# Queries and keys of the mixer made already turned, a pair of heads at a time, behind values and pooled channels

## Chip, core and metric

The kernel runs on one core of a Trainium2 chip. The metric is the device time of one execution in microseconds (us), lower is better. Engines are named as the profile names them: PE (TensorE) for matrix products, with PEld for its weight loads, DVE (VectorE), ACT (ScalarE), POOL (GpSimd), and SP, which issues most of the transfers.

## What is computed

A decoder layer on 256 tokens of width 1024: a SwiGLU FFN (width 2816), a token mixer, a second FFN, each with RMS normalisation and with shift, scale and gate from a conditioning vector.

```python
h = h + 0.5 * gt1 * swiglu(modulate(rmsnorm(h, g_ffn1), sh1, sc1), w1_gate, w1_up, w1_down)
n = modulate(rmsnorm(h, g_mix), sh2, sc2)
u, q, k, v = split(n @ w_in)                 # 512 columns each
y_pool = multiscale_pool(u, w_pool, pool_scale)   # 4 groups of 128 channels, windows 2, 4, 8, 16
y_attn = dilated_attention(q, k, v)               # 8 heads of 64, causal, ALiBi, 3 dilated branches
h = h + gt2 * (concat([y_pool, y_attn]) @ w_out)
h = h + 0.5 * gt3 * swiglu(modulate(rmsnorm(h, g_ffn2), sh3, sc3), w2_gate, w2_up, w2_down)
return rmsnorm(h, g_final)
```

## The kernel before

The 256 tokens are two tiles (t = 0, 1) of 128. Every large product is made of three products in a rounded 32-bit type: each operand is split into a high part and a rest, and hi*hi, lo*hi and hi*lo are summed. Weights come as units of 1 MB (128 x 2048 floats), in the order that `plan()` writes out; SP loads them into four buffers (`raw`), and for each half of a unit ACT makes the high part (L293) and DVE the rest (L294). A unit of kind "ada" is not a weight of PE: DVE reduces it with the conditioning vector, two reductions a unit (L282, with its read-out), to columns of shift, scale and gate. `weave` puts these units between the others; `WMIX` says from which unit of the mixer on. A load waits until the buffer that it takes is free, which means DVE is done with it.

The order on each engine is written by a scheduler from the code's order and from priorities (`urgent`); `order_dep` and `line_up` add orders by hand around the normalisations.

The mixer begins with the normalised tokens, turned so that the model width is on partitions: `nm[t]`, as high part and rest. They live in one of three homes (`homes`, `new_n`): two in `rounded`, one in `third`; the mixer's result `y[t]` takes a home too. `zchunk(ci, t)` makes 512 columns of `w_in` for one token tile: the tokens are the stationary operand, 512 columns of weights stream, 24 products of 512 rows, then ACT copies the result out (L742). Chunks come in the order q0, k0, q1, k1, v0, v1, u0, u1. `turn_heads(t)` turns q and k of a tile (eight PE transposes, L321, names `tq`, `tk`) and ACT copies them to `qT`, `kT` (L847). For a pair of heads hp, `scores` makes the products (PE, L760, `sc`), DVE adds the bias and takes the minimum (L771), ACT the exponential (L773), DVE divides (L775, L777); `heads_turn` turns the probabilities (L787, `pt`, copied by ACT at L790 to `pts`), `heads_out` multiplies them with the values (L799, `yt`), and ACT and DVE write high part and rest to y (L802, L804). These steps stand between products of the later chunks. `pool_group(g)` makes two small products and writes y (L810 to L823). `wout(t, ...)` is the output product (L890, `accm`), 48 products a tile. `finish2(t)` adds the gated result to `h` (L343, L345), sums squares on ACT (L348) and DVE (L351), and POOL takes the root (L354); ACT and DVE scale the rows (L356, L357, `xsc`), PE turns them (`xtc`), and the second FFN's first products (`le`, L522) begin.

In the FFNs, from chunk 6 (first) and 4 (second) on, `block` works the other way: 128 columns of weights are stationary, and `rounded` streams for both tiles at once, 512 rows (high part and rest of both tiles) against the weights' high part and 256 against their rest.

Of the kernel before, what the change touches and what calls it, by code (L numbers as in the profile page):

```python
# [15 lines left out]
P = 128  # L16
S = 256
# [25 lines left out]
WMIX = (4, 12)  # L43
# [16 lines left out]
def plan():  # L60
# [33 lines left out]
    mix = [("win", (ci, h)) for ci in (1, 2, 3, 0) for h in range(2)] + [("wout", i) for i in WOUT]  # L94
# [8 lines left out]
def pack(inp):  # L103
# [14 lines left out]
    for i, (kind, a) in enumerate(order):  # L118
# [58 lines left out]
def block_kernel(ctx, tc, w, vec, x, c, gf, wpool, bandd, biasd, out):  # L177
# [150 lines left out]
    homes = iter((0, 1, 2, 1, 2, 0, 0, 1))  # L328
# [106 lines left out]
    def block(f, ci, b, hh, hl):  # L435

        his, los = want("gu", (f, ci, b))
        ps = [psp.tile([P, 2 * S], F32, name=f"bl{f}_{ci}_{b}{e}", tag="ps") for e in range(2)]
        for k in range(KD):
            for e in range(2):  # L440
                mm(ps[e], his[k // 4][:, ts(k % 4 * 2 + e, P)], rounded[:, k].rearrange("p a t c -> p (a t c)"),  # L441
                   start=k == 0, stop=False)
        for k in range(KD):
            for e in range(2):
                mm(ps[e][:, 0:S], los[k // 4][:, ts(k % 4 * 2 + e, P)], rounded[:, k, 0].rearrange("p t c -> p (t c)"),  # L445
                   start=False, stop=k == KD - 1)
        with urgent():
# [246 lines left out]
    def finish1(t):  # L694
        with urgent():
            if t == 0:
                scale_cols(1, SC2)
            xs = norm_rows(t, f"b{t}", nm["acc"][t], nm["g"],
                           (place["win", (1, 1)] + 0.5 if t == 0 else place["win", (3, 0)], place["win", (1, 0)] + 1))
        def after(steps, gate=GATE):  # L700
            nm[t] = norm_mod(xs, 1, SH2, f"b{t}", step=steps[gate])
            if t == 1:
                r0, m0, r1, m1 = [chain[f"b{u}", kind] for u in range(NT) for kind in ("rows", "mod")]
                soon = [halves_of([("win", (1, 1)), ("win", (2, 0))], e)[1:] for e in range(2)]
                late = [halves_of([("win", (2, 1))], e) for e in range(2)]
# [24 lines left out]
    def zchunk(ci, t, scale=1.0, between={}):  # L730
# [10 lines left out]
        with urgent():  # L741
            nc.scalar.activation(z, ps, AF.Copy, scale=scale)  # L742
# [51 lines left out]
    def heads_out(hp, v, y):  # L794
        pts = turned_p[hp]
        ps = psp.tile([P, S], F32, name=f"yt{hp}", tag="ps")
        for t, cs, qs in ((0, slice(0, S), slice(0, S)), (1, slice(P, S), slice(S, 384))):
            for e in range(2):
                mm(ps[e * DH:e * DH + DH, cs], v[t][:, ts(2 * hp + e, DH)], pts[e][:, qs], start=t == 0, stop=t == 1)  # L799
        with urgent():  # L800
            for t in range(NT):
                nc.scalar.copy(y[t][0][:, slot(t, 4 + hp), :], ps[:, ts(t, P)])  # L802
            for t in range(NT):
                nc.vector.tensor_tensor(y[t][1][:, slot(t, 4 + hp), :], ps[:, ts(t, P)],  # L804
                                        y[t][0][:, slot(t, 4 + hp), :].bitcast(F32), ALU.subtract)

    def pool_group(g, u, y):
# [10 lines left out]
        with urgent():  # L818
            sc = psc[:, g:g + 1]
            for t in range(NT):  # L820
                nc.scalar.activation(y[t][0][:, slot(t, g), :], p2[:, ts(t, P)], AF.Copy, scale=sc)
            for t in range(NT):
                nc.vector.scalar_tensor_tensor(y[t][1][:, slot(t, g), :], p2[:, ts(t, P)], sc,  # L823
                                               y[t][0][:, slot(t, g), :].bitcast(F32), ALU.mult, ALU.subtract)
# [87 lines left out]
    wout(0, (0, 1))  # L912
# [91 lines left out]
```

## Time and profile before

| what | value |
|---|---|
| time, median of 3 runs (lowest to highest) | 475.97 us (475.29 to 476.56) |
| the profiled execution's own time | 478.23 us |
| its span, first to last instruction | 476.4 us |
| PE busy | 465.5 us (98%) |
| DVE busy | 372.3 us (78%) |
| ACT busy | 276.1 us (58%) |
| granted TensorE clock, mean | 0.996 |
| mixer, first w_in product to first product of the second FFN | 200.64 to 285.15 us |

The busy times are shares of the whole span. In rows of the timeline the first column is the start from the span's start, the second the length; consecutive matmuls overlap, so the time that one takes of PE is the distance to the next start. "x8" is a run of eight like it. A bracket says how long the engine was idle before the row, and what ended that.

### The profile page before, as it was taken

What the parts mean: (1) busy time and instruction counts of PE and PEld (TensorE: products, weight loads), DVE (VectorE), ACT (ScalarE), POOL (GpSimd) and SP (SyncE); (2) the same over time, 40 slices, a digit from 0 to 9 for tenths busy, and PEclk for the clock granted to TensorE, in tenths of its full rate; (3) what the DMA queues carried; (4) which work ended last, traced back from release to release, by engine and by line L of the source; (5) the groups of instructions that cost most, each with busy time, mean ns of one, the idle gap of its engine ahead of it and who ended that gap; (6) DMA issues with size and microseconds to landing.
All of it is one profiled execution on the core that took longest, in us unless ns stands there. A gap on an engine that the chain in (4) does not pass through costs nothing.

```text
span 476.4 us, 6380 instructions
## 1 busy us (share of the span) xinstructions
PE 465.5 (98%) x2327; PEld 387.7 (81%) x2327; DVE 372.3 (78%) x616; ACT 276.1 (58%) x488; POOL 13.5 (3%) x35
## 2 busy tenths in 40 slices
PE   8899999999999999999999999999999999999994
PEld 4678888888888888888878888888888888888883
DVE  4988899997989995689999868967876766666344
ACT  4666586444556563886877478847545554655211
POOL 1000000000000000120001000000000000000010
PEclk9999999999999999999999999999999999999998
DMA  8999896799789976568986974986678755550002
GB/s 280 421 342 354 286 362 256 291 411 420 268 310 378 352 281 246 207 216 327 378 295 258 371 259 178 369 316 252 229 270 296 264 177 182 191 203 1 2 4 84
DMA packets 19105, 126.09 MB, mean 265 GB/s; under 512 B 2217, under 2 KB 2753, under 8 KB 4738
## 3 DMA queue, kind: packets, MB, share of 16 engines
q1 hardware_dynamic: 17568, 121.18, 67.4%
q0 software_dynamic: 1216, 3.98, 2.4%
q10 hardware_dynamic: 290, 0.53, 0.3%
q8 instruction: 18, 0.29, 0.2%
q14 instruction: 13, 0.11, 0.1%
HBM read 124.62 MB, written 1.06 MB: 264 GB/s over the span
## 4 chain that ended last, share of the span: by engine, by line
PE 79%; DMA 7%; DVE 5%; ACT 5%; issue 2%; SPq 1%; POOL 1%; POOLq 0%; DVEq 0%; ACTq 0%
PE accf L473 22%; PE bl L441 18%; PE bl L445 10%; PE le L522 9%; DMA raw<-in_w_dram 7%; PE ld L522 6%; PE accm L890 5%; ACT hi L293 2%; PE sh L405 2%; PE ld L405 2%; DVE lo L294 1%; DVE raw L282 1%; PE ht L427 1%; PE sh L406 1%; PE ld L406 1%
## 5 line engine op out<-in xcount | busy, mean ns | idle before, releaser
L294 DVE TENSOR_TENSOR lo<-raw,hi 128x1024 fp32r<-128x1024 f32 (+1 forms) x158 | 184.2, 1193 | 40.8 <-ACT hi L293 24.2
L293 ACT CAST hi<-raw 128x1024 fp32r<-128x1024 f32 (+1 forms) x158 | 158.8, 1031 | 66.7 <-DMA raw<-in_w_dram 35.0
L441 PE MATMUL bl<-rounded,hi 128*128 128x512 f32 x384 | 91.5, 390 | 0.0
L282 DVE CUSTOM_DVE_ANT_0 raw<-raw,cb,h 128x1024 f32<-128x1024 f32 x70 | 88.2, 1278 | 2.2 <-DMA raw<-in_w_dram 2.2
L441 PEld LDWEIGHTS bl<-rounded,hi 128*128 128x128 f32 x384 | 71.1, 188 | 14.1
L473 PE MATMUL accf<-hi,hh 128*128 128x512 f32 x172 | 54.5, 392 | 0.0
L473 PE MATMUL accf<-hi,hl 128*128 128x512 f32 x172 | 54.1, 390 | 0.0
L473 PE MATMUL accf<-lo,hh 128*128 128x512 f32 x172 | 54.0, 389 | 0.0
L445 PEld LDWEIGHTS bl<-rounded,lo 128*128 128x128 f32 x384 | 49.2, 191 | 1.9
L445 PE MATMUL bl<-rounded,lo 128*128 128x256 f32 x384 | 49.8, 283 | 0.0
L473 PEld LDWEIGHTS accf<-lo,hh 128*128 128x128 f32 x172 | 32.3, 188 | 6.8
L473 PEld LDWEIGHTS accf<-hi,hl 128*128 128x128 f32 x172 | 32.2, 188 | 6.7
L473 PEld LDWEIGHTS accf<-hi,hh 128*128 128x128 f32 x172 | 31.5, 188 | 5.9
L522 PE MATMUL le<-hi,rounded 128*128 128x512 f32 x128 | 32.4, 390 | 0.0
L451 ACT COPY sg<-bl 128x256 f32<-128x256 f32 x24 | 8.9, 373 | 37.5 <-PE bl L445 37.5
L522 PE MATMUL ld<-hi,rounded 128*128 128x512 f32 x112 | 29.1, 397 | 0.7 <-ACT rounded L500 0.7
L522 PEld LDWEIGHTS le<-hi,rounded 128*128 128x128 f32 x128 | 24.0, 188 | 4.9
L522 PEld LDWEIGHTS ld<-hi,rounded 128*128 128x128 f32 x112 | 20.7, 188 | 6.9 <-ACT rounded L500 2.1
L405 PE MATMUL zp<-hi,third 128*128 128x512 f32 x64 | 20.3, 398 | 0.0
L405 PE MATMUL zp<-hi,rounded 128*128 128x512 f32 x64 | 20.1, 396 | 0.0
L453 ACT ACTIVATE sg<-sg 128x256 f32<-128x256 f32 x24 | 10.1, 420 | 14.9 <-DVE sg L452 14.7
L522 PE MATMUL le<-lo,rounded 128*128 128x512 f32 x64 | 17.6, 389 | 0.0
(195 smaller groups left out, 556.5 us busy)
## 6 DMA issues: line engine op xcount, KB each, us to landing
raw<-in_w_dram SPq DMA_DIRECT2D x112, 1024.0 KB, 6.2
raw<-in_w_dram SPq DMA_DIRECT2D x4, 512.0 KB, 8.4
gt<-gd POOLq DMA_DIRECT2D x3, 512.0 KB, 6.9
bias<-in_bias_dram POOLq DMA_DIRECT2D x2, 512.0 KB, 3.7
h<-in_x_dram SPq DMA_DIRECT2D x1, 576.0 KB, 4.6
band_all<-in_band_dram POOLq DMA_DIRECT2D x1, 544.0 KB, 4.8
h<-in_x_dram SPq DMA_DIRECT2D x1, 512.0 KB, 3.7
gfb<-in_gf_dram POOLq DMA_DIRECT2D x1, 512.0 KB, 11.2
```

Of the source, the lines that this page charges most:

```text
L282: note(nc.vector.tensor_tensor_reduce(r, r, cb, 1.0, vecs[:, m:m + 1], ALU.mult, ALU.add, mod[:, m:m + 1]), i, 1)
L293: note(nc.scalar.copy(hi[:, o:o + n], src), i + s / 2, 0)
L294: note(nc.vector.tensor_tensor(lo[:, o:o + n], src, hi[:, o:o + n].bitcast(F32), ALU.subtract), i + s / 2, 0)
L405: return [mm(ps, nh[:, k, :], whi, start=first, stop=False), mm(ps, nl[:, k, :], whi, start=False, stop=False), mm(ps, nh[:, k, :], wlo, s ...
L406: mm(ps, nh[:, k, :], wlo, start=False, stop=last)]
L441: mm(ps[e], his[k // 4][:, ts(k % 4 * 2 + e, P)], rounded[:, k].rearrange("p a t c -> p (a t c)"), start=k == 0, stop=False)
L445: mm(ps[e][:, 0:S], los[k // 4][:, ts(k % 4 * 2 + e, P)], rounded[:, k, 0].rearrange("p t c -> p (t c)"), start=False, stop=k == KD - 1)
L451: nc.scalar.copy(dst, src[:, S:2 * S])
L453: nc.scalar.activation(sg, sg, AF.Silu)
L473: steps.append(mm(accs[b], a, cols(ww, 2 * k + b), start=st, stop=sp))
L522: done.append(mm(banks[ci][t], n[t][a][:, j, :], cols(ww, lead_set(f, j).index(ci)), start=j == 0 and p == 0, stop=last and p == 2))
L890: steps.append(mm(acc2[t][b], a[:, slot(t, k), :], cols(ww, 2 * kk + b), start=st, stop=sp))
```

## The change

Values and pooled channels come first, as chunks like before: v0, u0, v1, u1. Queries and keys follow as four blocks of the FFN's kind (`heads_in(hp)`): a unit "qk" holds the 128 columns of q and the 128 columns of k of one pair of heads; weights stay, and `rounded` streams for both tiles, so q and k come out turned. ACT copies the half that comes of the tokens' rest, scaled, and DVE adds the other half onto it into `qT`, `kT`. The attention steps of pairs 0 to 2 stand between the two halves of later blocks; the rest of them between pool groups and inside `wout(0)`. Since blocks read `rounded` for both tiles, `nm` takes the homes 0 and 1; y of tile 0 takes home 0 after that, y of tile 1 takes `third`, and the first heads' y of tile 0, written before the last block is done, has a tile of its own (`y_first`). The modulation units come one place earlier in the weight order.

```diff
-WMIX = (4, 12)
+WMIX = (3, 11)
...
-    mix = [("win", (ci, h)) for ci in (1, 2, 3, 0) for h in range(2)] + [("wout", i) for i in WOUT]
+    mix = [("win", (ci, h)) for ci in (3, 0) for h in range(2)] + [("qk", hp) for hp in range(4)]
+    mix += [("wout", i) for i in WOUT]
...
+        elif kind == "qk":
+            w[i].reshape(P, KD, 2, P)[:] = win[:, :, :, 1:3, P * a:P * a + P].transpose(2, 0, 1, 3, 4).reshape(P, KD, 2, P)
...
-    homes = iter((0, 1, 2, 1, 2, 0, 0, 1))
+    homes = iter((0, 1, 0, 0, 2, 1, 0, 1))
...
+    def weights_stay(unit, ps, between=None):
+        his, los = unit
         for k in range(KD):
             for e in range(2):
                 mm(ps[e], his[k // 4][:, ts(k % 4 * 2 + e, P)], rounded[:, k].rearrange("p a t c -> p (a t c)"),
                    start=k == 0, stop=False)
+        if between:
+            between()
         for k in range(KD):
             for e in range(2):
                 mm(ps[e][:, 0:S], los[k // 4][:, ts(k % 4 * 2 + e, P)], rounded[:, k, 0].rearrange("p t c -> p (t c)"),
                    start=False, stop=k == KD - 1)
...
-    def turn_heads(t):
-        def go():
-            pts = [turn(z[f"{name}{t}"], f"t{name}{t}") for name in "qk"]
-            with urgent():
-                for dst, pt in zip((qT, kT), pts):
-                    nc.scalar.copy(dst[:, :, ts(t, P)], pt)
...
-    z["q0"] = zchunk(1, 0, QS)
-    z["k0"] = zchunk(2, 0, 1.0, {AFTER1: lambda: after(nm["steps"], 5)})
-    z["q1"] = zchunk(1, 1, QS, {3: turn_heads(0)})
-    z["k1"] = zchunk(2, 1, 1.0)
-    z["v0"] = zchunk(3, 0, 1.0, {3: turn_heads(1), 6: go((0, 0), (0, 1))})
-    z["v1"] = zchunk(3, 1, 1.0)
-    z["u0"] = zchunk(0, 0, 1.0, {1: go((1, 0)), 3: go((2, 0), (0, 2)), 7: go((1, 1))})
-    z["u1"] = zchunk(0, 1, 1.0, {1: go((2, 1), (0, 3)), 4: go((1, 2)),
-                                 6: lambda: (go((2, 2))(), nm.update(g2=gate_rows(GT2, 1.0)))})
-    for g in range(4):
-        pool_group(g, (z["u0"], z["u1"]), y)
-        if g == 1:
-            heads_turn(3)
-    heads_out(3, (z["v0"], z["v1"]), y)
+    y_first = xp.tile([P, 2, P], F32R, name="y_first")
+    def yk(t, k, e):
+        return y_first[:, e, :] if (t, k) == (0, 4) else y[t][e][:, k, :]
...
+    def heads_in(hp, between=None):
+        ps = [accp.tile([P, 2 * S], F32, name=f"qk{hp}{e}", tag="acc") for e in range(2)]
+        weights_stay(want("qk", hp), ps, between)
+        with urgent():
+            for e, (dst, scale) in enumerate(((qT, QS), (kT, 1.0))):
+                tmp = work.tile([P, S], F32, name=f"qk_rest{hp}{e}", tag="t2", bufs=T2)
+                nc.scalar.activation(tmp, ps[e][:, S:2 * S], AF.Copy, scale=scale)
+                nc.vector.scalar_tensor_tensor(dst[:, hp, :], ps[e][:, 0:S], scale, tmp, ALU.mult, ALU.add)
...
+    z["v0"] = zchunk(3, 0)
+    z["u0"] = zchunk(0, 0, {AFTER1: lambda: after(nm["steps"], 5)})
+    z["v1"] = zchunk(3, 1)
+    z["u1"] = zchunk(0, 1)
+    heads_in(0)
+    heads_in(1, go((scores, 0)))
+    heads_in(2, go((heads_turn, 0), (scores, 1)))
+    heads_in(3, go((heads_out, 0), (heads_turn, 1), (scores, 2)))
+    nm["g2"] = gate_rows(GT2, 1.0)
+    for g in range(2):
+        pool_group(g)
+    go((heads_out, 1), (heads_turn, 2), (scores, 3))()
+    for g in range(2, 4):
+        pool_group(g)
+    heads_out(2)
...
-    wout(0, (0, 1))
+    wout(0, (0, 1), None, {2: lambda: heads_turn(3), 3: lambda: heads_out(3)})
```

What the scheduler makes of it, at three places. First PE, where q and k of tile 1 were turned before (inside the chunk v0; `tq`, `tk` are the transposes):

```order
L406 MATMUL zp_2134<-lo_1_1780,third 128x512
L321 MATMUL tq_2158<-ident,z_2105 128x128 x4
L321 MATMUL tk_2163<-ident,z_2132 128x128 x4
L405 MATMUL zp_2134<-hi_1_1779,third 128x512 x2
L406 MATMUL zp_2134<-lo_1_1780,third 128x512
```

and now, in the second block (`qk_2181`, `qk_2182` are its q and k), where the scores of pair 0 stand between high and low weights:

```order
L443 MATMUL qk_2181<-rounded,hi_1_1942 128x512
L443 MATMUL qk_2182<-rounded,hi_1_1942 128x512
L769 MATMUL sc_2213<-kT,qT 128x128
L769 MATMUL sc_2214<-kT,qT 128x128
L769 MATMUL sc_2213<-kT,qT 128x256
L769 MATMUL sc_2214<-kT,qT 128x256
L449 MATMUL qk_2181<-rounded,lo_0_1939 128x256
L449 MATMUL qk_2182<-rounded,lo_0_1939 128x256
```

The transposes are gone, and what stands between the products is the scores, which need DVE's additions of the block before.

Second, the last pair's scores. On PE they stood ahead of the last pooled chunk's later products (`yt_2404` is `heads_out(1)`, `sc` the scores of pair 3):

```order
L799 MATMUL yt_2404<-pts_2387,z_2255 64x256
L799 MATMUL yt_2404<-pts_2393,z_2255 64x256
L799 MATMUL yt_2404<-pts_2387,z_2282 64x128
L799 MATMUL yt_2404<-pts_2393,z_2282 64x128
L760 MATMUL sc_2413<-kT,qT 128x128
L760 MATMUL sc_2414<-kT,qT 128x128
L760 MATMUL sc_2413<-kT,qT 128x256
L760 MATMUL sc_2414<-kT,qT 128x256
L405 MATMUL zp_2400<-hi_0_1959,rounded 128x512 x2
```

and now they stand between pool groups, behind three early output products (`accm`) and the turn of pair 2:

```order
L808 MATMUL yt_2488<-pts_2398,z_2098 64x128
L808 MATMUL yt_2488<-pts_2404,z_2098 64x128
L796 MATMUL pt_2497<-ident,p_2412 128x128 x3
L796 MATMUL pt_2503<-ident,p_2423 128x128 x3
L898 MATMUL accm_2573<-hi_0_2051,third 128x512 x2
L898 MATMUL accm_2572<-lo_0_2052,third 128x512
L769 MATMUL sc_2509<-kT,qT 128x128
L769 MATMUL sc_2509<-kT,qT 128x256
L769 MATMUL sc_2510<-kT,qT 128x128
L769 MATMUL sc_2510<-kT,qT 128x256
L819 MATMUL po_2537<-band_all,z_2071 128x128
```

Scores of pair 3 now follow `heads_out(1)` by a turn and three products. On DVE, the subtraction of `heads_out(1)` (`yt_2404`) and the minima of pair 3 (`p_2419`) stood behind one cast:

```order
L294 TENSOR_TENSOR lo_0_2180<-raw_2177,hi_0_2179 128x1024
L804 TENSOR_TENSOR rounded<-yt_2404,rounded 128x128
L804 TENSOR_TENSOR third<-yt_2404,third 128x128
L771 ISA p_2419,mx_2420<-sc_2413,bias_1921 128x128
L771 ISA mx_2420 128x1
L771 ISA p_2430,mx_2431<-sc_2414,bias_1921 128x128
```

and now (`yt_2488`, `p_2515`) behind two pool groups' subtractions, a reduction and a cast:

```order
L832 SCALAR_TENSOR_TENSOR rounded<-pw_2470,psc,rounded 128x128
L832 SCALAR_TENSOR_TENSOR third<-pw_2470,psc,third 128x128
L285 ISA raw_2183,mod<-raw_2183,cb,h 128x1024
L285 ISA mod 128x1
L832 SCALAR_TENSOR_TENSOR rounded<-pw_2482,psc,rounded 128x128
L832 SCALAR_TENSOR_TENSOR third<-pw_2482,psc,third 128x128
L297 TENSOR_TENSOR lo_0_2272<-raw_2269,hi_0_2271 128x1024
L813 TENSOR_TENSOR rounded<-yt_2488,rounded 128x128
L813 TENSOR_TENSOR third<-yt_2488,third 128x128
L780 ISA p_2515,mx_2516<-sc_2509,bias_1925 128x128
L780 ISA mx_2516 128x1
```

So between the pools and the minima DVE has more to do than before. 

Third, the third normalisation. DVE, the residual of tile 0 (`resc`) up to its sum of squares (L351) and the scaled rows (L357):

```order
L343 TENSOR_TENSOR resc_2676<-accm_2566,gt_2483 128x512
L343 TENSOR_TENSOR resc_2682<-accm_2567,gt_2483 128x512
L345 TENSOR_TENSOR h<-h,resc_2676 128x512
L345 TENSOR_TENSOR h<-h,resc_2682 128x512
L386 SCALAR_TENSOR_TENSOR acol<-mod,gains 128x1
L351 ISA resc_2682,vc_2685<-h,vc_2679 128x512
L351 ISA vc_2685 128x1
L357 TENSOR_SCALAR xsc_2690<-h,rc_2687 128x512
```

and now, where the same lines are L346 to L360:

```order
L346 TENSOR_TENSOR resc_2705<-accm_2570,gt_2462 128x512
L346 TENSOR_TENSOR resc_2711<-accm_2571,gt_2462 128x512
L348 TENSOR_TENSOR h<-h,resc_2705 128x512
L348 TENSOR_TENSOR h<-h,resc_2711 128x512
L285 ISA raw_2574,mod<-raw_2574,cb,h 128x1024
L285 ISA mod 128x1
L354 ISA resc_2711,vc_2714<-h,vc_2708 128x512
L354 ISA vc_2714 128x1
L285 ISA raw_2600,mod<-raw_2600,cb,h 128x1024
L285 ISA mod 128x1
L360 TENSOR_SCALAR xsc_2719<-h,rc_2716 128x512
```

Three reductions that stood ahead of the residual stand inside its chain or after it. On ACT, from the first products' inputs of the second FFN to tile 1's scaled rows (L348 the square, L356 the rows):

```order
L293 CAST hi_0_2629<-raw_2627 128x1024
L500 ACTIVATE rounded<-xT_2570,mod,acol 128x128 x2
L293 CAST hi_1_2633<-raw_2627 128x1024
L348 ACTIVATE resc_2763,vc_2766<-h 128x512
L356 ACTIVATE xsc_2776<-h,rc_2774 128x512
```

and now (L351 the square, L359 the rows):

```order
L509 ACTIVATE rounded<-xT_2703,mod,acol 128x128 x2
L296 CAST hi_0_2644<-raw_2642 128x1024
L351 ACTIVATE resc_2792,vc_2795<-h 128x512
L296 CAST hi_1_2648<-raw_2642 128x1024
L359 ACTIVATE xsc_2805<-h,rc_2803 128x512
```

One cast that stood ahead of the square stands behind it.

More of the change, by code (lines that the diff above doesn't have):

```diff
@@ L446, in block @@
                    start=False, stop=k == KD - 1)
+    def block(f, ci, b, hh, hl):
+        ps = [psp.tile([P, 2 * S], F32, name=f"bl{f}_{ci}_{b}{e}", tag="ps") for e in range(2)]
+        weights_stay(want("gu", (f, ci, b)), ps)
         with urgent():
@@ L698, in finish1 @@
             xs = norm_rows(t, f"b{t}", nm["acc"][t], nm["g"],
-                           (place["win", (1, 1)] + 0.5 if t == 0 else place["win", (3, 0)], place["win", (1, 0)] + 1))
+                           (place["win", (3, 1)] + 0.5 if t == 0 else place["qk", 0], place["win", (3, 0)] + 1))
         def after(steps, gate=GATE):
@@ L703, in after @@
                 r0, m0, r1, m1 = [chain[f"b{u}", kind] for u in range(NT) for kind in ("rows", "mod")]
-                soon = [halves_of([("win", (1, 1)), ("win", (2, 0))], e)[1:] for e in range(2)]
-                late = [halves_of([("win", (2, 1))], e) for e in range(2)]
+                soon = [halves_of([("win", (3, 1)), ("win", (0, 0))], e)[1:] for e in range(2)]
+                late = [halves_of([("win", (0, 1))], e) for e in range(2)]
                 line_up(r0[0], *soon[0], m0[0], *late[0], r1[0], m1[0])
@@ L728, in block_kernel, with zchunk @@
     xp = mix_pool.__enter__()
[L730 removed]
+    def zchunk(ci, t, between={}):
         ps, steps = accp.tile([P, 512], F32, name=f"zp{ci}{t}", tag="acc"), []
@@ L741, in zchunk @@
         with urgent():
-            nc.scalar.activation(z, ps, AF.Copy, scale=scale)
+            nc.scalar.copy(z, ps)
         return z
@@ L792, in heads_turn, with heads_out @@
         turned_p[hp] = pts
-    def heads_out(hp, v, y):
+    def heads_out(hp):
         pts = turned_p[hp]
@@ L866, in block_kernel @@
-    for g in range(4):
-        pool_group(g, (z["u0"], z["u1"]), y)
-        if g == 1:
-            heads_turn(3)
-    heads_out(3, (z["v0"], z["v1"]), y)
-    mix_pool.__exit__(None, None, None)
-    ffn2_pool = tc.tile_pool(name="ffn2", bufs=1, reuse_waits="tile")
-    fp[0] = ffn2_pool.__enter__()
+            for f, *a in calls:
+                f(*a)
+        return all_of_them
+    z["v0"] = zchunk(3, 0)
+    z["u0"] = zchunk(0, 0, {AFTER1: lambda: after(nm["steps"], 5)})
+    z["v1"] = zchunk(3, 1)
@@ L875, in block_kernel, with wout @@
+    z["u1"] = zchunk(0, 1)
[10 more added lines that the diff above has]
+    heads_out(2)
     acc2 = new_acc("m")
-    xT3 = fp[0].tile([P, 4, S], F32, name="xT3", tag="prl", bufs=2)
-    def wout(t, banks, after=None):
+    def wout(t, banks, after=None, between={}):
@@ L882, in wout @@
                 after(steps)
+            if n in between:
+                between[n]()
             hi, lo = want("wout", i)
-            yh, yl = y[t]
             for kk in range(2):
                 k = 2 * i + kk
-                for (a, ww, st, sp) in ((yh, hi, n + kk == 0, False), (yl, hi, False, False),
-                                        (yh, lo, False, n == 3 and kk == 1)):
+                for (e, ww, st, sp) in ((0, hi, n + kk == 0, False), (1, hi, False, False),
+                                        (0, lo, False, n == 3 and kk == 1)):
                     for b in banks:
-                        steps.append(mm(acc2[t][b], a[:, slot(t, k), :], cols(ww, 2 * kk + b), start=st, stop=sp))
+                        steps.append(mm(acc2[t][b], yk(t, k, e), cols(ww, 2 * kk + b), start=st, stop=sp))
     n3 = {}
@@ L910, in finish2 @@
         return after
-    wout(0, (0, 1))
+    wout(0, (0, 1), None, {2: lambda: heads_turn(3), 3: lambda: heads_out(3)})
+    mix_pool.__exit__(None, None, None)
+    ffn2_pool = tc.tile_pool(name="ffn2", bufs=1, reuse_waits="tile")
+    fp[0] = ffn2_pool.__enter__()
+    xT3 = fp[0].tile([P, 4, S], F32, name="xT3", tag="prl", bufs=2)
     after = finish2(0)
```

24 lines of the change are left out of this document (8 added, 16 removed).

## Prediction

> **What bounds the kernel now.** I read the page's busy times and chain first, then busy times by stretch over the mixer (from the first w_in product at 200.64 to the first product of the second FFN at 285.15), then TensorE's (PE's) timeline there, then VectorE (DVE), ScalarE (ACT) and the DMA queue in the same stretch.
>
> ```profile
> span 476.4 us, 6380 instructions
> PE 465.5 (98%) x2327; PEld 387.7 (81%) x2327; DVE 372.3 (78%) x616; ACT 276.1 (58%) x488; POOL 13.5 (3%) x35
> PE 79%; DMA 7%; DVE 5%; ACT 5%; issue 2%; SPq 1%; POOL 1%; POOLq 0%; DVEq 0%; ACTq 0%
> 200.64:285.15 84.51, 84.41 (x442) 67.84 (x441) 74.88 (x162) 61.29 (x137) 5.32 (x11) 1.00 0.80 302
> 224.43:246.60 22.17, 22.17 (x125) 17.55 (x124) 20.65 (x61) 16.68 (x41) 0.00 (x0) 1.00 0.89 355
> 246.60:256.29 9.69, 9.59 (x56) 6.92 (x55) 9.69 (x30) 8.11 (x22) 0.53 (x1) 1.00 0.73 265
> ```
>
> The last three rows read: length, busy PE, weight loads, DVE, ACT, POOL, granted clock, DMA share, GB/s. PE fills 84.41 of the mixer's 84.51 us at full clock, so time is won or lost by what PE streams and by the moments when it must wait. DVE is the second constraint: 20.65 of 22.17 us over values and the first pooled chunk, and all 9.69 us of the second pooled chunk, where the softmax runs. Whatever is late there will be late because of DVE.
>
> **What PE streams.** Rows are start, length, instruction; what counts is start to start, since matmuls overlap.
>
> ```profile
> 200.64 0.62 PE L405 MATMUL zp<-hi,third 128*128 128x512 f32 x2
> 206.08 0.62 PE L405 MATMUL zp<-hi,third 128*128 128x512 f32 x2
> 214.47 0.39 PE L406 MATMUL zp<-lo,rounded 128*128 128x512 f32 x1
> 214.70 0.60 PE L321 MATMUL tq<-ident,z 128*128 128x128 f32 x4
> 215.13 0.60 PE L321 MATMUL tk<-ident,z 128*128 128x128 f32 x4
> 215.49 0.71 PE L405 MATMUL zp<-hi,rounded 128*128 128x512 f32 x2
> 367.84 2.08 PE L445 MATMUL bl<-rounded,lo 128*128 128x256 f32 x16
> 369.76 3.82 PE L441 MATMUL bl<-rounded,hi 128*128 128x512 f32 x16
> 373.41 2.08 PE L445 MATMUL bl<-rounded,lo 128*128 128x256 f32 x16
> ```
>
> One chunk (24 products of 512 rows) takes 206.08 - 200.64 = 5.44, or 0.227 each. Queries and keys are four chunks, 21.76. The new form is the FFN's block: 16 of 512 rows (373.41 - 369.76 = 3.65) and 16 of 256 (369.76 - 367.84 = 1.92), 5.57 back to back. Four blocks are 22.28: **+0.52**. The streamed rows are the same in both (96 x 512 = 64 x 512 + 64 x 256); the 256-row products cost 0.120 instead of half of 0.227. The Trainium skill ("TensorE: Matmul & The Clock Gate", Back-to-back issue gap) gives N/2.4 + 2.5 ns, 215.8 and 109.2 ns, for isolated products. By it a block would cost only 0.02 more than a chunk and this term would be 0.08, the change 0.44 better; the rows above, with their weight loads, say otherwise and are used.
>
> The 16 transposes of q and k disappear: each set of eight takes 215.49 - 214.70 = 0.79, and the pair behind it is 0.71 long instead of 0.62. Two sets: **-1.76**. ACT's four copies of q and k chunks and its four copies of turned tiles go, and eight half-size copies come; ACT has room (61.29 of 84.51), so I cost that at nothing. DVE gets eight additions of 128x256, which nothing takes away; they are below.
>
> ```profile
> 238.62 0.82 PE L787 MATMUL pt<-ident,p 128*128 128x128 f32 x6
> 239.19 0.71 PE L405 MATMUL zp<-hi,third 128*128 128x512 f32 x2
> 240.74 0.87 PE L799 MATMUL yt<-pts,z 128*64 128x256 f32 x8
> 241.54 0.93 PE L760 MATMUL sc<-kT,qT 64*128 64x128 f32 x8
> 242.40 0.73 PE L405 MATMUL zp<-hi,third 128*128 128x512 f32 x2
> 247.06 0.39 PE L406 MATMUL zp<-lo,rounded 128*128 128x512 f32 x1
> 247.55 1.24 PE L799 MATMUL yt<-pts,z 128*64 128x256 f32 x8
> 248.71 0.93 PE L760 MATMUL sc<-kT,qT 64*128 64x128 f32 x8
> ```
>
> Turning probabilities costs 0.57, weighing values 0.80, scores of one pair 0.86, each plus about 0.1 at the switch. Scores of pairs 0 and 1 now go in separately: one switch more and a shorter run, **+0.2**. The second heads_out waited before: it starts 0.26 after the product ahead could end (247.06 + 0.23), and takes 1.16 instead of 0.80; less a usual switch of 0.08 that is 0.54, because ACT's copy of the turned probabilities came late. In the new order that copy has a half block more: **-0.54**. That gives -1.58 before any new wait.
>
> **New waits.** From block 1 to the last scores every hand-over runs through DVE, so I laid DVE's new order along the clock with these durations:
>
> ```profile
> 218.92 4.62 DVE L294 TENSOR_TENSOR lo<-raw,hi 128x1024 fp32r<-128x1024 f32 x4
> 223.47 1.28 DVE L282 CUSTOM_DVE_ANT_0 raw<-raw,cb,h 128x1024 f32<-128x1024 f32 x1
> 224.67 1.28 DVE L282 CUSTOM_DVE_ANT_0 raw<-raw,cb,h 128x1024 f32<-128x1024 f32 x1
> 243.53 0.28 DVE L804 TENSOR_TENSOR rounded<-yt,rounded 128x128 fp32r<-128x128 f32 x1
> 243.93 0.28 DVE L771 CUSTOM_DVE_ANT_0 p<-sc,bias 128x128 f32<-128x128 f32 x1
> 245.04 1.28 DVE L282 CUSTOM_DVE_ANT_0 raw<-raw,cb,h 128x1024 f32<-128x1024 f32 x1
> 247.57 1.00 DVE L777 TENSOR_SCALAR p<-p,rec 128x128 f32<-128x128 f32 x4
> 248.49 1.22 DVE L294 TENSOR_TENSOR lo<-raw,hi 128x1024 fp32r<-128x1024 f32 x1
> L964 DVE SCALAR_TENSOR_TENSOR o<-h,ro,gfb 128x256 f32<-128x256 f32 x4 | 1.8, 482 | 1.3 <-POOL ro L962 1.3
> 219.03 0.33 SPq L277 DMA_DIRECT2D raw<-in_w_dram  x1
> 226.37 2.00 ACT L293 CAST hi<-raw 128x1024 fp32r<-128x1024 f32 x2 [1.14 <-DMA raw<-in_w_dram]
> ```
>
> Start to start: a lo half 4.55/4 = 1.14, a modulation reduction ("ada", L282) 1.20, a pair's minima 1.11, its divisions 0.92, a y pair 0.40. No addition of the new form is in the trace: the nearest of its kind (L964) has 0.48 busy, and 0.40 start to start after its pipelined tail. PE's clock in the new order: block 0 starts at 223.53 (one transpose set less), block 1 at 229.1, block 2 at 235.6, block 3 at 242.8, pooling at 251.0. Before block 0's results can be added, DVE must do the low halves of the last qk unit's first part, whose load is about the twelfth of a full queue; the like load before took 226.37 - 219.03 = 7.3 us, so issued at 220.7 it lands at 228.0, and qT, kT of pair 0 are there at 231.0 (PE wants them at 232.7). From there to the y pair of heads 1, DVE has 8 lo halves, 5 reductions, 3 sets of minima and of divisions, 6 additions, and 4 pairs of subtractions (two of y, two of the pools, priced alike): 9.1 + 6.0 + 3.3 + 2.8 + 2.4 + 1.6 = 25.2, with reciprocals (about 0.1 a pair) 25.6, and about 1.2 of gates by ACT (block 1's end, the exponentials). On the way: divisions of pair 1 done 246.1 (PE turns them at 247.2), qT, kT of pair 2 at 246.9 (wanted 247.9), of pair 3 at 253.9 (their accumulators are reused by the output product at 254.1; scores at 257.3). Margins of about 1 us, none negative. Then the second score tile of pair 3 takes the PSUM buffer of heads_out(1), whose subtraction is done at 258.0 while PE stands there at 257.7: **+0.3**. Bounds: 0, and 1.2 for one reduction that slips ahead of it.
>
> The second wait is at the third normalisation.
>
> ```profile
> 285.15 1.98 PE L522 MATMUL le<-hi,rounded 128*128 128x512 f32 x8
> 291.05 1.03 PE L321 MATMUL xtc<-ident,xsc 128*128 128x128 f32 x8
> 286.22 1.07 ACT L293 CAST hi<-raw 128x1024 fp32r<-128x1024 f32 x1
> 287.16 0.66 ACT L348 ACTIVATE resc<-h 128x512 f32<-128x512 f32 x1
> 289.70 0.72 ACT L356 ACTIVATE xsc<-h,rc 128x512 f32<-128x512 f32 x1 [1.79 <-POOL rc L354]
> ```
>
> Tile 1's rows are ready at 289.70 + 0.72 = 290.42, and PE turns them at 291.05: 0.63 to spare, counted from the end of tile 0's output products. Six of tile 1's 48 products now stand among the pool groups, so PE comes 6 x 0.227 = 1.36 sooner; a reduction now stands ahead of the sum of squares (L351), 0.6 later after the part that waited for POOL anyway; one cast fewer stands ahead of ACT's square, 0.95 sooner (start to start, 286.22 to 287.16). 0.63 - 1.36 - 0.6 + 0.95 = -0.4: **+0.4**. Bounds: 0 and 1.2 (another cast in the way).
>
> Moved at no cost: SP's queue carries the same 1 MB units, with each reduction's unit one place earlier; the casts of the next units have 10 us and more ahead of use. The gate GT2's transpose stands right behind block 3 instead of inside the last pooled chunk, and its two POOL DMAs have the pool groups and the output products of tile 0 to land in; if they were late, the third normalisation would wait for them. The y rows of tile 0 now share a home with the normalised rows, and only pair 0's, in its own tile, are written before block 3 ends.
>
> Sum: -1.76 + 0.52 + 0.2 - 0.54 + 0.3 + 0.4 = **-0.88**. The profiled execution has 478.23 (2.3 above the median of the runs, its span 476.4), so 477.35 for its like; against the median, 475.97, **475.1**.
>
> **Rivals.**
> *Both waits stay hidden* (DVE 0.3 early, ACT's order no worse): -1.58, 474.4. For it: all other margins are positive. Against: DVE has no free time in the stretch where it matters.
> *DVE falls behind, slower.* Place: the turn of pair 1's probabilities to the scores of pair 3. DVE's work in a block is two lo halves, two reductions, minima, divisions, additions and a y pair: 2.3 + 2.4 + 1.1 + 0.9 + 0.8 + 0.4 = 7.9, PE's 6.5 to 8.1. If DVE is 3 us later than laid out (loads landing 3 us late, an addition costing 0.8), the 1.0 to 1.2 of margin are gone and 2 us more are paid: about +1.1, 477.1; it decides from 2 us of lateness on, where the gain is eaten. For it: DVE busy 9.69 of 9.69. Against: blocks use a weight unit up in 5.5 us, so buffers come free sooner.
> *The gain is hidden anyway*, because the weight stream sets the second FFN's pace:
>
> ```profile
> L293 ACT CAST hi<-raw 128x1024 fp32r<-128x1024 f32 (+1 forms) x158 | 158.8, 1031 | 66.7 <-DMA raw<-in_w_dram 35.0 <-PE accf L473 13.5 <-PE bl L441 10.3
> ```
>
> ACT's casts wait 35.0 us for loads; if PE's lead were used up, nothing would be left: 476.0. Against: the same casts also wait for PE to free buffers, so the stream is paced by PE.
>
> **How the numbers follow.** Forecast 0.5, hidden waits 0.2, DVE behind 0.18, gain hidden 0.12. A change of less than 0.3% (1.4 us) cannot be told from none here. Faster by more: the hidden-waits case and three tenths of the forecast's spread, 0.35. Slower by more needs 1.4 us of loss, the worse part of the DVE case: 0.13. Within 0.3%: 0.52. The range: the low end is the hidden-waits case less 0.6, by which the runs shown lie off their median (475.29 to 476.56), 473.8; the high end the DVE case, 477.2 rounded up.
>
> **What would show it.** Transposes of q and k gone and blocks of 5.5 to 5.6 in PE's timeline; no wait ahead of the scores of pairs 0 to 2; a short gap ahead of the second score tile of pair 3, released by DVE, and one ahead of tile 1's turn, released by ACT's xsc; the mixer 0.9 us shorter and the second FFN as long as before. A gap over 1 us ahead of any scores or turned probabilities, or blocks above 5.8, would make it wrong.

## The result, and the profile after

The changed kernel takes 479.17 us (median of 6 executions, 478.69 to 479.77), the kernel before beside it 475.84 (475.29 to 476.56; six executions, the first three of which gave the 475.97 above): ratio 1.0070, 95% interval 1.0059 to 1.0082, so 3.3 us slower (2.8 to 3.9). The forecast was 475.1 in a range of 473.8 to 477.2. Of its cases, "DVE falls behind" has the right sign, but what was lost was lost elsewhere. The profiled execution took 479.49, its span is 477.7.

First the page, then busy times by stretch (length, PE, weight loads, DVE, ACT, POOL, clock, DMA share, GB/s): the whole mixer, the part from the first pool group to tile 0's gated sum, and tile 1's output products up to the second FFN.

```profile
span 477.7 us, 6414 instructions
PE 466.4 (98%) x2343; PEld 388.0 (81%) x2343; DVE 375.2 (79%) x624; ACT 274.5 (57%) x488; POOL 15.3 (3%) x35
199.37:285.72 86.35, 84.97 (x459) 68.05 (x457) 77.19 (x168) 57.81 (x133) 7.06 (x11) 1.00 0.74 280
251.01:273.97 22.96, 22.48 (x132) 17.07 (x131) 19.59 (x53) 15.22 (x41) 1.65 (x3) 1.00 0.69 258
273.97:285.72 11.75, 10.85 (x53) 8.72 (x51) 11.22 (x19) 6.12 (x12) 2.49 (x2) 1.00 0.56 197
```

The mixer takes 86.35 instead of 84.51 us. PE was busy in all but 0.1 of it before; now it idles 1.38, all of it late, and POOL's busy time has grown though it has nothing more to do. The new products are what was forecast:

```profile
222.22 3.79 PE L443 MATMUL qk<-rounded,hi 128*128 128x512 f32 x16
225.84 2.08 PE L449 MATMUL qk<-rounded,lo 128*128 128x256 f32 x16
227.76 3.81 PE L443 MATMUL qk<-rounded,hi 128*128 128x512 f32 x16
231.50 0.93 PE L769 MATMUL sc<-kT,qT 64*128 64x128 f32 x8
```

A block takes 227.76 - 222.22 = 5.54 (5.57 said), block 0 starts 22.85 after the first w_in product (22.89 said), and the first scores start right behind block 1's high part. I then took PE's timeline of both kernels row by row and listed where a row took longer than its kind does undisturbed. Four places are new. **First, the scores of pair 2:**

```profile
238.78 0.93 PE L769 MATMUL sc<-kT,qT 64*128 64x128 f32 x8
239.64 0.39 PE L449 MATMUL qk<-rounded,lo 128*128 128x256 f32 x1
247.01 0.92 PE L769 MATMUL sc<-kT,qT 64*128 64x128 f32 x4
247.86 0.50 PE L449 MATMUL qk<-rounded,lo 128*128 128x256 f32 x2
248.29 0.92 PE L769 MATMUL sc<-kT,qT 64*128 64x128 f32 x4
257.46 1.11 PE L769 MATMUL sc<-kT,qT 64*128 64x128 f32 x8
258.50 0.38 PE L819 MATMUL po<-band_all,z 128*128 128x128 f32 x1
```

Pair 1 takes 0.86 for both heads (eight records). Pair 2 is written head by head, with two products of the block between; each head alone takes 0.85 (247.86 - 247.01, 249.14 - 248.29). With the second switch that is 0.95 lost, and no idle time shows it. My reading is that the second head's PSUM buffer is free later: scores, turned probabilities and heads_out share four buffers (`psp`), and block 3 asks for five in a row. a_sc and a_wlead below bear on that. Pair 3 takes 1.04; DVE's subtraction of heads_out(1), which frees the buffer that the prediction named there, ends within that run:

```profile
257.84 0.28 DVE L813 TENSOR_TENSOR third<-yt,third 128x128 fp32r<-128x128 f32 x1
```

**Second, the output products over the last heads:**

```profile
SPq L280 <- DVE lo L297: 13.3, 2, 8.9
251.56 9.58 SPq L280 DMA_DIRECT2D raw<-in_w_dram  x2
265.00:271.10 6.10, 6.10 (x35) 4.63 (x34) 5.39 (x11) 0.87 (x3) 0.00 (x0) 1.00 1.01 398
271.12 1.05 ACT L296 CAST hi<-raw 128x1024 fp32r<-128x1024 f32 x1 [3.78 <-DMA raw<-in_w_dram]
272.07 0.26 ACT L811 CAST rounded<-yt 128x128 fp32r<-128x128 f32 x1
271.29 0.62 PE L898 MATMUL accm<-lo,rounded 128*128 128x512 f32 x2
272.38 0.50 PE L898 MATMUL accm<-hi,rounded 128*128 128x512 f32 x1 [0.47 <-ACT rounded L811]
```

The cast of unit lead(1,1) stands ahead of the heads' casts (L811) on ACT and waits for its load. SP issued no load between 251.56 and 260.81 (the second row is two issues of 0.33, 9.58 from the start of the one to the end of the other), because it waited for buffers that DVE was not done with (first row, SP's waits from 251.5 to 262: two for a low half, the longest 8.9); after that the transfers ran full (third row: share 1.01, 398 GB/s), and the load, issued at 261.98, landed at 271.1. PE starts 0.64 late (271.29 + 2 x 0.227 = 271.74).

**Third, the third normalisation of tile 0; fourth, that of tile 1:**

```profile
274.14 1.28 DVE L346 TENSOR_TENSOR resc<-accm,gt 128x512 f32<-128x512 f32 x2
276.54 1.28 DVE L285 CUSTOM_DVE_ANT_0 raw<-raw,cb,h 128x1024 f32<-128x1024 f32 x1
276.93 0.94 POOL L352 TENSOR_TENSOR vc<-vc,deps 128x1 f32<-128x1 f32 x1 [15.92 <-ACT resc L351]
277.90 0.75 DVE L354 CUSTOM_DVE_ANT_0 resc<-h,vc 128x512 f32<-128x512 f32 x1
278.58 1.28 DVE L285 CUSTOM_DVE_ANT_0 raw<-raw,cb,h 128x1024 f32<-128x1024 f32 x1
278.74 1.55 POOL L357 TENSOR_TENSOR rc<-vc,mhalf 128x1 f32<-128x1 f32 x1 [0.87 <-DVE vc L354]
280.32 0.72 ACT L359 ACTIVATE xsc<-h,rc 128x512 f32<-128x512 f32 x1 [3.55 <-POOL rc L357]
281.10 0.66 PE L324 MATMUL xtc<-ident,xsc 128*128 128x128 f32 x4 [0.90 <-ACT xsc L359]
288.92 0.62 ACT L351 ACTIVATE resc<-h 128x512 f32<-128x512 f32 x1
292.19 0.98 PE L324 MATMUL xtc<-ident,xsc 128*128 128x128 f32 x7 [0.42 <-ACT xsc L359]
```

And the like rows of the kernel before, tile 0:

```profile
273.35 1.29 DVE L343 TENSOR_TENSOR resc<-accm,gt 128x512 f32<-128x512 f32 x2 [0.36 <-PE accm L890]
276.14 0.19 POOL L349 TENSOR_TENSOR vc<-vc,deps 128x1 f32<-128x1 f32 x1 [15.63 <-ACT resc L348]
277.20 0.57 POOL L354 TENSOR_TENSOR rc<-vc,mhalf 128x1 f32<-128x1 f32 x1 [0.87 <-DVE vc L351]
277.81 0.73 ACT L356 ACTIVATE xsc<-h,rc 128x512 f32<-128x512 f32 x1 [1.81 <-POOL rc L354]
```

From sum to scaled rows it takes 6.18 (274.14 to 280.32) instead of 4.46. Two reductions (L285) now run inside, and POOL's two operations of 128x1, 0.19 and 0.57 before, take 0.94 and 1.55: the first ends about with the reduction beside it (276.54 + 1.28 = 277.82), the second 0.43 behind the other one (279.86). PE comes 1.07 late (the bracket, and the pipeline's tail). The turn is also split by a product: with the two products in and behind it, it takes 1.40 (281.10 to 282.50) where the unsplit turn before took 1.33 (279.28 to 280.61), 0.07 more. (The expectations below still count 0.18 for the split, both switches of it; a turn in one piece has one of them too.) Tile 1's turn is 0.57 late. No reduction stands in tile 1's chain; ACT's square for it (288.92) stands behind an unbroken row of ACT's work that begins with tile 0's late rows at 280.32.

### The profile page after: what moved, and what is told of

It reads as the page before. It is cut to its first block, busy times and chain, and to the rows that moved or that the text cites. A ratio compares the mean times of both kernels' runs of the same rounds, so it can differ in the third digit from the quotient of the medians.

```text
span 477.7 us, 6414 instructions
## 1 busy us (share of the span) xinstructions
PE 466.4 (98%) x2343; PEld 388.0 (81%) x2343; DVE 375.2 (79%) x624; ACT 274.5 (57%) x488; POOL 15.3 (3%) x35
## 4 chain that ended last, share of the span: by engine, by line
PE 87%; DMA 5%; ACT 3%; DVE 2%; issue 1%; SPq 1%; POOL 1%; POOLq 0%; DVEq 0%
PE accf L482 25%; PE bl L443 18%; PE bl L449 10%; PE ld L531 8%; PE le L531 8%; DMA raw<-in_w_dram 5%; PE qk L443 3%; PE zp L408 3%; PE qk L449 2%; PE sh L408 2%; PE zp L409 2%; PE ld L408 2%; ACT hi L296 1%; PE ht L430 1%; PE sc L769 1%
## 5 line engine op out<-in xcount | busy, mean ns | idle before, releaser
L285 DVE CUSTOM_DVE_ANT_0 raw<-raw,cb,h 128x1024 f32<-128x1024 f32 x70 | 88.4, 1279 | 0.1
L461 DVE TENSOR_TENSOR sg<-bl,sg 128x256 f32<-128x256 f32 x24 | 10.1, 421 | 9.2 <-ACT sg L460 8.8
```

The lines of the kernel that those rows point to most:

```text
L285: note(nc.vector.tensor_tensor_reduce(r, r, cb, 1.0, vecs[:, m:m + 1], ALU.mult, ALU.add, mod[:, m:m + 1]), i, 1)
L461: nc.vector.tensor_tensor(dst, src[:, 0:S], dst, ALU.add)
```

## Experiments

Runs whose names begin with a_ change the changed kernel, those with b_ the kernel before. Stretches in the table are read from PE's timeline: the mixer (first w_in product to the second FFN's first), and "lead" (from there to the second FFN's first block). From that block to the last output product every run took 138.2 to 138.3. "Against before" sets mixer and lead against 84.33 + 44.41, the means of four profiles: two of the kernel before (mixer 84.51, 83.80) and its variants b_wlead and b_heads (84.56, 84.46), whose mixer has the steps in the same places. The timed difference comes from the ratio to runs of the kernel before on the same chip, 1.001 being 0.48 us.

| kernel | median us | ratio (95%) | timed difference us | mixer | lead | against before |
|---|---|---|---|---|---|---|
| changed | 479.17 | 1.0070 (1.0059 to 1.0082) | +2.8 to +3.9 | 86.35 | 45.06 | +2.7 |
| a_y7 | 478.65 | 1.0050 (1.0033 to 1.0067) | +1.6 to +3.2 | 85.76 | 45.10 | +2.1 |
| a_gfb | 478.32 | 1.0040 (1.0026 to 1.0055) | +1.2 to +2.6 | 85.64 | 45.07 | +2.0 |
| a_noada | 478.10 | 1.0039 (1.0020 to 1.0059) | +1.0 to +2.8 | 84.50 | 46.03 | +1.8 |
| a_sc | 477.84 | 1.0044 (1.0023 to 1.0065) | +1.1 to +3.1 | 85.03 | 44.62 | +0.9 |
| a_wlead | 476.77 | 1.0012 (0.9998 to 1.0026) | -0.1 to +1.2 | 85.40 | 44.44 | +1.1 |
| a_sw | 474.98 | 0.9973 (0.9960 to 0.9987) | -1.9 to -0.6 | 83.63 | 44.41 | -0.7 |
| b_wlead | 476.02 | 0.9994 (0.9982 to 1.0007) | -0.9 to +0.3 | 84.56 | 44.41 | |
| b_heads | 476.68 | 1.0007 (0.9993 to 1.0021) | -0.3 to +1.0 | 84.46 | 44.42 | |

**The kernel before, a second profile.**

> The kernel before, unchanged, a second profile. Its first profiled execution took 478.23 us, 2.4 above the median of its timed runs. Theory 'a late start': that profile lost time ahead of the mixer (its first w_in product at 200.64, that of the changed kernel at 199.37, although the code up to there is the same), so a second profile has the first w_in product near 199.4, and the mixer again 84.5 long. Rival 'the mixer itself was slow in that profile': the second one has a mixer clearly shorter than 84.5, and the change costs the mixer more than the 1.84 (86.35 to 84.51) that the two profiles show.

It took 475.38. Two rows of it, the mixer and its second heads_out:

```profile
198.49:282.29 83.80, 83.80 (x442) 67.37 (x441) 74.86 (x162) 61.36 (x137) 5.32 (x11) 1.00 0.79 305
245.18 0.87 PE L799 MATMUL yt<-pts,z 128*64 128x256 f32 x8
```

Both theories hold in part. The mixer starts 2.15 earlier than in the first profile, in code that the change doesn't touch, and it is 0.71 shorter. The second heads_out is followed by the scores after 0.80 (245.98), where the first profile had 1.16: the wait of 0.54 that I counted as removed is not in every execution (the profiles of b_wlead and b_heads have it).

**The last heads' casts ahead of the late unit.**

```diff
+    order_dep(casts[("lead", (1, 1)), 0][0], y_last[0], "heads first")
```

Here `y_last` holds the second of the last heads' two result casts (L811).

> The changed kernel, with ACT's high-part cast of unit lead(1,1) (L296) put behind the casts of the last heads' result (L811). In the changed kernel's trace that cast waits 3.78 us for its load, the two result casts stand behind it, and the output product over them starts 0.64 late (272.38; 271.29 + 2 x 0.227 = 271.74). Theory 'the cast is only in the way': the gap goes, nothing else moves, 479.17 - 0.64 = 478.5. Rival 'the load sets the pace anyway': the cast's low half and the third normalisation behind it on DVE come no earlier, the time moves into the wait ahead of xtc (0.90 now), 479.2.

The gap is gone, and PE goes on 0.80 behind the start of the heads' products:

```profile
269.94 0.87 PE L810 MATMUL yt<-pts,z 128*64 128x256 f32 x8
270.74 0.98 PE L902 MATMUL accm<-hi,rounded 128*128 128x512 f32 x3
280.95 0.44 PE L324 MATMUL xtc<-ident,xsc 128*128 128x128 f32 x2 [1.03 <-ACT xsc L359]
```

The mixer is 0.59 shorter, the wait ahead of tile 0's turn 0.13 longer: the first theory, with a small part of the rival. The times (478.65 for 479.17) agree but, at their width, would not show it alone.

**Why the load was late.** In a_gfb a broadcast of 512 KB is issued later:

```diff
-    nc.gpsimd.dma_start(gfb, gf.to_broadcast([P, D]))
+    gfb_load = nc.gpsimd.dma_start(gfb, gf.to_broadcast([P, D]))
+    order_dep(gfb_load.ins, chain["c1", "rows"][0][0], "after the third norm")
```

> The changed kernel, with the broadcast of the last norm's gain (gfb, 512 KB, issued by POOL at 260.47) put behind tile 1's rows in the third normalisation; its scaling on ACT (L945) moves behind too. In the changed kernel the load of lead(1,1), issued at 261.98, landed at 271.1, 9.1 later, and between 265.0 and 271.1 the transfers moved 398 GB/s at a share of 1.01. Theory 'the transfers are full': half a MB less is 1.3 us at 398 GB/s, the load lands near 269.8, its cast is done ahead of the last heads' result (270.24), the gap of 0.64 goes: 478.5. Rival 'the load is late because it was issued late, and would take 9 anyway': no change, 479.2. In both the third normalisation waits as before (1.07 and 0.57).

```profile
269.07 1.05 ACT L296 CAST hi<-raw 128x1024 fp32r<-128x1024 f32 x1 [2.42 <-DMA raw<-in_w_dram]
269.57 1.21 PE L898 MATMUL accm<-hi,rounded 128*128 128x512 f32 x4
```

The cast waits 2.42 instead of 3.78, 1.36 less for half a MB less (1.3 said), and the gap is gone. So the transfers were full and set when the load landed; that the loads were asked for so late and so close together goes with SP's wait for buffers above.

**No reduction in tile 0's normalisation.**

```diff
-                           (place["lead", (1, 1)] + 0.5, place["lead", (1, 2)]) if t == 0 else
+                           (place["lead", (1, 1)] + 0.5, place["lead", (1, 0)]) if t == 0 else
...
-            n3[t] = norm_mod(xs, 2, SH3, f"c{t}", t, xT3, steps[GATE])
+            n3[t] = norm_mod(xs, 2, SH3, f"c{t}", t, xT3, steps[31 if t == 0 else GATE])
```

> As a_y7, and DVE's modulation reductions of the units ahead of lead(1,1) and lead(1,2) (L285) put behind the scaling of tile 0's rows in the third normalisation; the turn of tile 0 keeps its place in the order. In the changed kernel's trace the chain from the gated sum to xsc takes 6.18 us (274.14 to 280.32) instead of 4.46; one reduction stands between the sum and the squares on DVE, and POOL's two small operations beside reductions take 0.94 and 1.55 instead of 0.19 and 0.57, each ending within 0.5 of the end of the reduction beside it. Theory 'a reduction holds POOL up': with none beside them they take 0.19 and 0.57 again, the chain 4.5, the waits of PE ahead of xtc of tile 0 go (1.07 and 0.18 for the split turn): about 1.2 less than a_y7, 477.3; in tile 1, where the second reduction of the unit ahead of lead(1,2) now runs beside POOL's addition, that one is the long one. Rival 'POOL is slow for a reason of its own' (its transfers, its place in the program): it stays 0.94 and 1.55, the chain shortens by the reduction's own time only, at most 0.6 less than a_y7.

Tile 0 (first two rows), then tile 1:

```profile
276.51 0.19 POOL L352 TENSOR_TENSOR vc<-vc,deps 128x1 f32<-128x1 f32 x1 [15.04 <-ACT resc L351]
277.57 0.57 POOL L357 TENSOR_TENSOR rc<-vc,mhalf 128x1 f32<-128x1 f32 x1 [0.88 <-DVE vc L354]
...
288.81 1.28 DVE L285 CUSTOM_DVE_ANT_0 raw<-raw,cb,h 128x1024 f32<-128x1024 f32 x1
289.12 1.02 POOL L352 TENSOR_TENSOR vc<-vc,deps 128x1 f32<-128x1 f32 x1 [10.98 <-ACT resc L351]
292.37 0.87 PE L324 MATMUL xtc<-ident,xsc 128*128 128x128 f32 x6 [1.37 <-ACT xsc L359]
```

POOL is back at 0.19 and 0.57 in tile 0, whose turn no longer waits (mixer 1.26 shorter than in a_y7). In tile 1 the addition that was 0.19 has become 1.02, beside the reduction that moved there, and PE waits 1.37. So what is beside it decides, not the place, and most of the gain went to the other tile. The expectation named that long addition, but priced it at nothing: 477.3 said, 478.10 measured. The Trainium skill ("SBUF — State Buffer", SBUF: two separate sides) says that VectorE and GpSimd share a pair of SBUF ports as an exclusive lock, and that an operation of VectorE with two inputs in SBUF blocks one of GpSimd that reads SBUF until it is done. The rows agree: three POOL operations issued beside a reduction ended only about when it did, or after it.

**The heads of pair 2 together.**

```diff
-    heads_in(3, go((heads_out, 0), (heads_turn, 1), (scores, 2)))
+    heads_in(3, go((heads_turn, 1), (scores, 2), (heads_out, 0)))
```

> The changed kernel, with heads_out(0) behind scores(2) in block 3 instead of ahead of heads_turn(1). In the changed kernel the score products of pair 2 stand head by head, with two products between them; each head alone takes 0.85 where both heads together take 0.86 in pairs 0 and 1: about 0.95 lost. In this order PE has pair 2's four products in one run, both heads in turn; the cast of lead(1,1) also stands behind the last heads' result, as in a_y7. Theory 'two heads share PE': pair 2 takes 0.86 again, and with the y gap gone (0.64) the time is 479.17 - 0.95 - 0.64 = 477.6. Rival 'the split only filled a wait for a PSUM buffer': a wait of up to 0.9 stands ahead of the scores instead and the time is about a_y7's, 478.5.

```profile
246.54 0.93 PE L769 MATMUL sc<-kT,qT 64*128 64x128 f32 x8
247.40 0.85 PE L449 MATMUL qk<-rounded,lo 128*128 128x256 f32 x5
```

With heads_out(0) behind them the two heads stand together, the pair takes 0.86 (247.40 - 246.54), and no wait stands in front, so the split was not just filling one. (The scheduler's order for this edit also puts the cast of lead(1,1) behind the last heads' result by itself.) All score products together take 3.43 instead of 4.46. The mixer is 0.73 shorter than in a_y7; tile 0's turn waits 0.17 more than there.

Why is a head alone as long as two? Two variants of the kernel before ask that. In b_heads the products of a pair are written head by head (the loop over heads outside), without anything between:

> The kernel before, with the score products written head by head (both products of one head, then both of the other) instead of the two heads in turn; nothing else moves. One head alone took 0.85 in the changed kernel (pair 2, split), both heads in turn 0.86. Theory 'two heads share PE as long as they alternate': in this order only the long product of the first head and the short one of the second overlap; the changed kernel's pair 3, which has this order, took 1.04. So 1.04 to 1.15 for a pair instead of 0.86, four pairs, about 0.9 more in all: 476.8. Rival 'the 0.85 of the split heads was a wait that the records do not name': no change, 0.86 for a pair, 475.9.

In b_rows the first heads of pairs 0 and 1 are neighbours, then the second ones (execution 476.82, beside 476.17):

> The kernel before, with the sixteen score records of pairs 0 and 1 in the order head 0 (pair 0), head 0 (pair 1), head 1 (pair 0), head 1 (pair 1): neighbours on the same 64 partitions stand together, then those on the other 64. With the two heads of a pair as neighbours, in turn or one behind the other, the sixteen took 1.62 (1.51 in the first profile of the kernel before); one head alone took 0.85 in the changed kernel. Theory 'neighbours on different 64 partitions overlap': two heads on the same 64 don't, so the sixteen take 2.4 to 3.4. Rival 'each head takes 0.43 and the lone one paid 0.42 for the switch to the next weights': 1.62 again.

The pair of b_heads, and the sixteen of b_rows:

```profile
240.26 0.93 PE L760 MATMUL sc<-kT,qT 64*128 64x128 f32 x8
241.12 0.50 PE L405 MATMUL zp<-hi,third 128*128 128x512 f32 x1
...
227.08 2.34 PE L761 MATMUL sc<-kT,qT 64*128 64x128 f32 x16
229.35 0.50 PE L405 MATMUL zp<-hi,third 128*128 128x512 f32 x1
```

In b_heads the pair still takes 0.86, so my theory that heads must alternate fell, and pair 3's 1.04 in the changed kernel has another cause. The sixteen of b_rows take 2.27 instead of 1.51 to 1.62, a little under the span that I gave: if only the middle two, on different partitions, overlap, that is three times 0.76. So heads on different 64 partitions overlap when they are neighbours, in either order, and the price of a split is a whole head. That the array takes such products concurrently is in the Trainium skill ("TensorE: Matmul & The Clock Gate", Packing small matmuls — row/col tiling).

**Everything at once.** The modulation units stand two places later in a_wlead (the changed kernel) and in b_wlead (the kernel before); a_sw has a_sc's edit as well:

```diff
-WLEAD = (0, 4)
+WLEAD = (2, 6)
```

> The changed kernel, with the last four modulation units two places later in the weight order: behind lead(1,2) to lead(1,5) instead of behind lead(1,0) to lead(1,3) (WLEAD). No reduction then stands between gated sum and xsc in either tile's third normalisation, and the units lead(1,1) and lead(1,2) are loaded one and two places sooner. Theory 'reductions and loads': POOL's operations 0.19 and 0.57 in both tiles, no wait ahead of xtc in either (1.07 + 0.18 and 0.57 now), and, the load of lead(1,1) being there in time, no gap ahead of the output product of heads 3 (0.64): 479.17 - 1.25 - 0.57 - 0.64 = 476.7. Rival 'the reductions only move': they come due at the fifth lead products and hold those up by 1 or more: 477.5 to 478.5.

> As a_wlead, and heads_out(0) behind scores(2) as in a_sc, so that the scores of pairs 2 and 3 have both heads in turn. Theory 'the ledger': the waits and splits that were found add up to the whole loss; 476.7 less 0.95 for pair 2 and 0.25 for pair 3: 475.5, within 0.2% of the kernel before (475.84). Rival 'a cost in the blocks themselves that the waits hide': it stays above 476.5.

> The kernel before, with its last four modulation units two places later in the same way. Its third normalisation has no reduction inside in either tile and PE does not wait ahead of xtc. Theory 'that place mattered only after the change': no difference, 475.8 give or take 0.5. Rival 'later modulation units are better anyway': 1 us or more faster, and then what a_wlead gains would be no repair of the change. Its profile also shows a third time whether the second heads_out waits (0.54 lost in the first profile of the kernel before, nothing in the second).

a_wlead came out at 476.77 (476.7 said): POOL's operations are 0.19 and 0.56 in tile 0, nothing waits ahead of tile 1's turn, the heads' gap is gone; a wait of 0.51 is left ahead of tile 0's turn, which the scheduler put six products earlier there. Pair 2 is still split in it, and the second head now waits:

```profile
247.70 0.92 PE L769 MATMUL sc<-kT,qT 64*128 64x128 f32 x4 [0.16 <-ACT pts L799]
```

ACT's copy of pair 1's turned probabilities is nothing that the scores of pair 2 read, so what they waited for can hardly be anything but a buffer: that is the most direct sign of the shortage. a_sw came out at 474.98 (475.5 said). Its mixer, and then the whole list of what PE waited for in this execution, a single wait outside the mixer:

```profile
198.27:281.90 83.63, 83.62 (x458) 67.61 (x457) 73.25 (x160) 59.06 (x137) 5.31 (x11) 1.00 0.73 279
PE spin L571 <- POOL ident masks.py:199: 1.4, 1, 1.4
```

PE waits nowhere in the mixer any more. The control b_wlead shows no difference from the kernel before, so the later modulation units repair something that only the change had broken. a_sw is faster than the kernel before by 0.13 to 0.40%, and so than both.

## Why the prediction was wrong

- **What PE streams** was right in kind: blocks 5.54 (5.57), transposes gone, no wait ahead of the scores of pairs 0 and 1. Products and transposes of q, k, v and u, with the second normalisation's turn of tile 1, take 45.8 of PE's time instead of 47.6 to 47.9, more of a gain than the terms gave (-1.76 + 0.52). The rival that DVE falls behind between pair 1's turn and pair 3's scores did not come: no such gap.
- **"Moved at no cost" and the third normalisation of tile 0,** which has no term at all, failed by the largest single amount. The reduction "ahead of the sum of squares" was costed for tile 1. It stands in tile 0's chain, as the DVE order ahead of the prediction shows. With POOL held up beside it and the next one, the chain is 1.72 longer, more than the 1.20 of a reduction, and PE loses 1.14 there. a_noada shows it in both tiles.
- **The price of a pair's scores, 0.86,** failed for pair 2. For it I asked only whether qT and kT would be there in time (they were), not whether PSUM had two free buffers at that point. The split cost 0.95; a_sc gave 0.73 of it back. The +0.2 for pairs 0 and 1 was about right: without the split, in a_sw, all score products take 0.16 more than before. At pair 3 0.18 of the expected +0.3 is there (1.04 for 0.86), at the place that was named; that it is the buffer is not shown, as no bracket stands inside the run.
- **"The casts of the next units have 10 us and more ahead of use"** failed. True for their use, but a cast that waits for its load stops what stands behind it on ACT, here the last heads' result: 0.64. Both a_y7 and a_gfb removed it.
- **Tile 1's turn**, +0.4 said, is 0.57, and that this is near was luck. One term of that sum, the reduction, is not in tile 1's chain. ACT works without a break from tile 0's rows to tile 1's square, 8.60 (280.32 to 288.92) where it was 9.35 (277.81 to 287.16). So the 2.51 that tile 0's rows come later goes on to tile 1, less 0.75 for the cast that moved.
- **The old wait ahead of the second heads_out, -0.54,** is in three of four profiles, so as a mean it was 0.4.

Together: -0.88 + 0.95 + 0.64 + 1.14 - 0.12 + 0.17 + 0.14 = +2.04, against +2.7 by the stretches and 2.8 to 3.9 timed. About 0.7 is left over, and a_sw shows where it sits. PE waits nowhere in its mixer, and yet that is only 0.70 shorter than the mean of the four profiles, where the terms without new waits gave -1.58. I added up, by kind, the time from each row's start to the next and set it against that mean. Products and transposes of q, k, v and u are 1.81 shorter (1.24 said), heads_out 0.34 shorter (0.54 said), scores 0.16 longer (0.2 said). But the 96 output products take 0.71 more (23.22 for 22.51), and turned probabilities, pool groups and the gate 0.59 more (7.10 for 6.51). **The prediction has no term for these last two, 1.30 together.** Why they are longer is not shown. A run of output products behind another kind of product takes about 0.1 more, and there are nine such runs instead of seven, which can be a part only.

So the repair of all four places (a_sw) ended at 474.98, near the forecast of 475.1, by luck: the forecast holds 0.7 of waits that a_sw does not have, and lacks the 1.30.

## What to carry to other kernels

When a change moves work, lay out every in-order engine through the places that follow, for each tile apart. Ask of each instruction that can wait for a load what stands behind it, and of each small POOL operation on a critical chain which long DVE operation may run beside it. Count free PSUM buffers where two products belong together: a scheduler that fills the wait turns it into a split that no list of waits shows. Steps that move to stand between other products change what those products cost, so price both places. And take a second profile of the kernel before, ahead of counting a wait as gain.

## What was not expected of the hardware

- A DVE reduction over 128x1024 held up POOL operations on 128x1 to about its own end or up to 0.43 beyond: 0.19 became 0.94 to 1.02, 0.57 became 1.55, back to 0.19 and 0.57 with nothing beside.
- Score products on 64 partitions overlap if neighbours lie on different 64: one head 0.85, two heads 0.86, sixteen records 1.51 to 1.62, or 2.27 with neighbours on the same half.
- With 1.5 us between runs ahead of the mixer, where the code is the same (first w_in product 198.27 to 199.80 in the changed kernel's variants), single profiles don't carry a difference of 0.3%; stretches that begin at a common product do.
